# Infinity norm of rows: the last piece reduced alone, the other partial results joined beside it, and both stores issued by SyncE

## Chip, cores, metric

One core of one Trainium2 chip. The time is the device time in microseconds of one execution. Ratios are the mean time of one kernel's fast runs over the mean of the other's fast runs of the same rounds, so they are not quite the ratio of the medians quoted beside them.

The **tail**: the time from the landing of the last load (the last of the sixteen steps of its semaphore in the trace) to the end of the span. Its last part is the **closing block**: the event semaphores and drains that the engines run after the last store has landed.

## The reference

```python
x = np.random.randn(8192, 8192).astype(np.float32)
out = np.linalg.norm(x, ord=np.inf, axis=1)     # out[row] = max over 8192 columns of |x[row, col]|
```

## The kernel before

268 MB are loaded once, in tiles of 128 rows (or 256 rows as two per partition), and reduced along the row. VectorE takes the absolute maximum in one instruction. Near the end ScalarE and GpSimd help: ScalarE writes absolute values in place, GpSimd takes a maximum over them. The last tile is cut into six pieces of falling size, so that little work is left after the last load.

```python
    + [[(16384, (3712, 3680))], [(8192, (2016, 1984))]]
    + [[(3872, (1696,)), (1952, (832,)), (1024, (416,)), (544, (192,)), (384, ()), (416, ())]]
# (columns of a piece, (columns of it that ScalarE + GpSimd take)); the rest is VectorE's
WARM = {-2: (4, 4, 4), -1: (4,), 0: (4,), 1: (2,)}   # matmuls on zeros and ones after a piece
# ... cut ...
    last = single.tile([P, w_last + n_part_last], FP32)  # last piece AND 9 partial results, side by side
# ... cut: the loop over pieces ...
            if final:
                for r in range(2):
                    keep(nc.scalar.copy(sb_pairs[:, :, r], ps_pairs[r]))
                absmax(res[:, R - 1 :], last)             # 416 columns and 9 partials in one reduce
            elif u == len(TILES) - 1:
                # ... transposes of the finished rows, when h == 0 ...
                red = shared(last, w_last + n_part, buf, w, g)
                n_part += 1 + len(g)
                warm(red, WARM.get(h, ()))
# ... cut ...
    nc.tensor.transpose(ps_ones, res[:, X_ONE:], ident)   # [128, 4] -> [4, 128]
    keep(nc.scalar.copy(sb_ones, ps_ones))
    keep(nc.scalar.dma_start(out=out[X_ONE * P :].rearrange("(r p) -> r p", p=P), in_=sb_ones))
    nc.sync.dma_start(out=out[: X_ONE * P].rearrange("(g p r) -> g p r", p=P, r=2), in_=sb_pairs)
```

The results lie one per partition, 128 partitions wide; the transposes put them into rows, so that a store has few long runs. Pieces are counted from 0 below; piece 4 is the last but one, piece 5 the last.

## Time and profile before

| | before |
|---|---|
| time, median of 6 runs | 628.24 us (627.88 to 628.37) |
| profiled run, span | 628.42 us, 626.6 us |
| DMA | 268.47 MB, mean 428 GB/s over the span |
| last load lands | 623.11 us |
| tail | 3.50 us |

In the windows view, the columns are the stretch, its length, then the busy time (and instructions) of PE, PEld, DVE, ACT and POOL, then the granted clock, the DMA share and GB/s.

```profile
623.90:624.00 0.10, 0.07 (x1) 0.08 (x1) 0.00 (x0) 0.00 (x0) 0.00 (x0) 0.94 0.08 21
624.00:624.10 0.10, 0.10 (x1) 0.01 (x1) 0.00 (x0) 0.00 (x0) 0.00 (x0) 0.50 0.00 0
```

The clock falls to half at 623.99, while the last transpose (623.92 to 624.27) is running.

### The profile page before, as it was taken

Reading aid. Unit: us, or ns where it says so; the run is one execution under the profiler, and the core shown is the slowest. Engines: PE = TensorE matmul, PEld = TensorE weight load, DVE = VectorE, ACT = ScalarE, POOL = GpSimd, SP = SyncE. Lnnn points to the kernel's source line nnn. Section 1 sums busy time; section 2 is a strip of 40 time slices with the busy share of each in tenths; the row PEclk is TensorE's granted clock in tenths of the full one; section 3 lists DMA queues with packets and bytes.
Section 4 is the critical chain, followed back from the end, with each engine's and each line's share of the span. In section 5 each row is a group of like instructions: output and inputs, shape, how many; then the busy total and the mean of one; then the engine's idle time right before and its main releaser. Section 6 shows DMA issues by size and latency. Waiting matters only on the chain.

```text
span 626.6 us, 212 instructions
## 1 busy us (share of the span) xinstructions
PE 8.1 (1%) x15; PEld 3.0 (0%) x15; DVE 536.8 (86%) x40; ACT 15.6 (2%) x13; POOL 14.6 (2%) x16
## 2 busy tenths in 40 slices
PE   0000000000000000000000000000000000000005
PEld 0000000000000000000000000000000000000001
DVE  1938988889888899888898888988889888899888
ACT  0000000000000000000000000000000000000044
POOL 0000000000000000000000000000000000000026
PEclk9999999999999999999999999999999999999999
DMA  8999999999999999999999999999999999999997
GB/s 368 435 469 402 469 402 469 402 469 402 464 406 464 406 456 414 431 439 427 443 410 460 406 464 402 469 402 469 402 464 406 464 406 464 406 460 410 439 410 291
DMA packets 5669, 268.47 MB, mean 428 GB/s; under 512 B 643, under 2 KB 933, under 8 KB 1317
## 3 DMA queue, kind: packets, MB, share of 16 engines
q1 hardware_dynamic: 5661, 268.47, 99.2%
q10 hardware_dynamic: 8, 0.00, 0.0%
HBM read 268.44 MB, written 0.03 MB: 428 GB/s over the span
## 4 chain that ended last, share of the span: by engine, by line
DMA 71%; DVE 28%; SPq 0%; issue 0%; PE 0%; ACT 0%; DVEq 0%
DMA ring<-in_x_dram 71%; DVE res L75 28%; DVE last L75 1%; SPq L147 0%; PE ps_ones L189 0%; ACT sb_ones L190 0%; DVEq L75 0%
## 5 line engine op out<-in xcount | busy, mean ns | idle before, releaser
L75 DVE TENSOR_REDUCE res<-ring 128x2 f32<-128x16384 f32 (+1 forms) x32 | 525.4, 16420 | 86.8 <-DMA ring<-in_x_dram 86.8
L97 ACT ACTIVATE ring<-ring 128x3712 f32<-128x3712 f32 (+7 forms) x8 | 13.5, 1712 | 575.9 <-DMA ring<-in_x_dram 572.6
L82 POOL TENSOR_REDUCE part<-ring 128x1 int32<-128x3712 int32 (+3 forms) x4 | 10.1, 2563 | 586.0 <-ACT ring L97 586.0
L118 PE MATMUL ps_warm<-ident 128*128 128x512 f32 (+1 forms) x12 | 7.5, 764 | 614.5 <-DVE part L75 613.2
L118 PEld LDWEIGHTS ps_warm<-ident 128*128 128x128 f32 x12 | 2.7, 258 | 618.4 <-issue 615.3
L75 DVE TENSOR_REDUCE part<-ring 128x1 f32<-128x800 f32 (+1 forms) x2 | 5.5, 2748 | 0.1
L75 DVE TENSOR_REDUCE last<-ring 128x1 f32<-128x2176 f32 (+4 forms) x5 | 5.3, 1115 | 0.1
L82 POOL TENSOR_REDUCE last<-ring 128x1 int32<-128x1696 int32 (+3 forms) x4 | 3.3, 842 | 0.5 <-ACT ring L97 0.4
L110 ACT ACT_TABLE_LOAD x1 | 1.3, 1283 | 31.6 <-DVE res L75 31.6
L104 POOL MEMSET ident<- 128x128 f32 x1 | 0.2, 206 | 21.5 <-DVE res L75 21.5
L75 DVE TENSOR_REDUCE res<-last 128x1 f32<-128x425 f32 x1 | 0.6, 595 | 0.1
L161 ACT COPY sb_pairs<-ps_pairs 30x128 f32<-30x128 f32 x2 | 0.4, 252 | 0.0
L82 POOL TENSOR_REDUCE res<-part 128x1 int32<-128x3 int32 x2 | 0.4, 200 | 0.1
L167 PE MATMUL ps_pairs<-ident,res 128*30 128x128 f32 x2 | 0.4, 272 | 0.0
L189 PE MATMUL ps_ones<-ident,res 128*4 128x128 f32 x1 | 0.3, 348 | 1.7 <-DVE res L75 1.7
masks.py:199 POOL TENSOR_SCALAR_AFFINE_SELECT ident<-ident 128x128 f32<-128x128 f32 x1 | 0.3, 295 | 0.1
L190 ACT COPY sb_ones<-ps_ones 4x128 f32<-4x128 f32 x1 | 0.3, 255 | 1.5 <-PE ps_ones L189 1.5
L167 PEld LDWEIGHTS ps_pairs<-ident,res 128*30 128x30 f32 x2 | 0.2, 106 | 0.6 <-issue 0.6
L110 ACT ACTIVATE ident<-ident 128x1 f32<-128x1 f32 x1 | 0.2, 203 | 0.0
L211 POOL MEMSET const-float32-0.0<- 128x1 f32 x1 | 0.1, 99 | 0.2 <-issue 0.2
L211 POOL MEMSET const-bfloat16-1.0<- 128x1 bf16 x1 | 0.1, 102 | 0.0
L211 POOL MEMSET const-uint8-127<- 128x1 uint8 x1 | 0.1, 102 | 0.0
(2 smaller groups left out, 0.2 us busy)
## 6 DMA issues: line engine op xcount, KB each, us to landing
ring<-in_x_dram SPq DMA_DIRECT2D x3, 4096.0 KB, 21.6
ring<-in_x_dram SPq DMA_DIRECT2D x1, 1936.0 KB, 35.4
ring<-in_x_dram SPq DMA_DIRECT2D x1, 976.0 KB, 37.3
ring<-in_x_dram SPq DMA_DIRECT2D x1, 512.0 KB, 38.1
ring<-in_x_dram SPq DMA_DIRECT2D x30, 40.8
ring<-in_x_dram SPq DMA_DIRECT2D x1, 272.0 KB, 38.3
last<-in_x_dram SPq DMA_DIRECT2D x1, 208.0 KB, 38.3
ring<-in_x_dram SPq DMA_DIRECT2D x1, 192.0 KB, 38.3
```

Of the source, the lines that this page charges most:

```text
L75: return keep(nc.vector.tensor_reduce(out=dst, in_=src, axis=X, op=MAX, apply_absolute_value=True,))
L82: keep(pool.add_instruction(mybir.InstTensorReduce(name=nc.get_next_instruction_name(), ins=[pool.lower_ap(src.bitcast(INT32))], outs=[poo ...
L97: keep(nc.scalar.activation(buf[:, a : a + c], buf[:, a : a + c], ABS))
L104: not_before(nc.gpsimd.memset(ident, 0.0), after, "not before the first row is in")
L110: keep(nc.scalar.activation(ident[:, :1], ident[:, :1], ABS)),
L118: keep(nc.tensor.matmul(ps_warm[:, : w * P], lhsT=ident, rhs=ident.unsqueeze(1).to_broadcast([P, w, P]), start=True, stop=True,)),
L161: keep(nc.scalar.copy(sb_pairs[:, :, r], ps_pairs[r]))
L167: keep(nc.tensor.transpose(ps_pairs[r], both[:, :, r], ident))
L189: nc.tensor.transpose(ps_ones, res[:, X_ONE:], ident)
L190: keep(nc.scalar.copy(sb_ones, ps_ones))
L211: nc = _bacc.Bacc("TRN2", target_bir_lowering=False, num_devices=1)
```

## The change

Its intent: VectorE's last reduce should not wait for the nine partial results. It takes the last piece alone; GpSimd joins the nine meanwhile. The two columns are transposed one after the other, and VectorE takes the maximum of the two rows in one partition. The three finished single rows are transposed and copied earlier, so the last store is one row of 512 values; SyncE issues both stores. Some columns move between pieces, and two warm-ups are added.

```diff
-    + [[(16384, (3712, 3680))], [(8192, (2016, 1984))]]
-    + [[(3872, (1696,)), (1952, (832,)), (1024, (416,)), (544, (192,)), (384, ()), (416, ())]]
+    + [[(16384, (3712, 3680))], [(8192, (1952, 1920))]]
+    + [[(3872, (1728,)), (1952, (832,)), (1056, (448,)), (576, (224,)), (352, ()), (384, ())]]
-WARM = {-2: (4, 4, 4), -1: (4,), 0: (4,), 1: (2,)}
+WARM = {-2: (4, 4, 4), -1: (4,), 0: (4,), 1: (2,), 2: (2,), 4: (1,)}
 ... (tiles: parts apart from last; end[0..1], ps_end[0..1]; ps_ones and sb_ones in one partition)
             if final:
-                for r in range(2):
-                    keep(nc.scalar.copy(sb_pairs[:, :, r], ps_pairs[r]))
-                absmax(res[:, R - 1 :], last)
+                copied = keep(nc.scalar.copy(sb_ones[:, : (n_ones - 1) * P], ps_ones))
+                not_before(nc.sync.dma_start(out=..., in_=sb_pairs), copied, "out of the way of the loads")
+                absmax(end[0], last)
+                max_pool(end[1], parts)
 ... (piece 0: transposes of three single rows added; the pairs' copies moved here)
-    nc.tensor.transpose(ps_ones, res[:, X_ONE:], ident)
-    keep(nc.scalar.copy(sb_ones, ps_ones))
-    keep(nc.scalar.dma_start(out=..., in_=sb_ones))          # four rows of 128, ScalarE
-    nc.sync.dma_start(out=..., in_=sb_pairs)
+    keep(nc.tensor.transpose(ps_end[1], end[1], ident))
+    keep(nc.scalar.copy(sb_last, ps_end[1]))
+    keep(nc.tensor.transpose(ps_end[0], end[0], ident))
+    keep(nc.vector.tensor_tensor(out=sb_ones[:, (n_ones - 1) * P :], in0=ps_end[0], in1=sb_last, op=MAX))
+    nc.sync.dma_start(out=out[X_ONE * P :].rearrange("(o p) -> o p", o=1), in_=sb_ones)   # one row of 512
```

More of the change, by code (lines that the diff above doesn't have):

```diff
@@ L58 @@
     sb_pairs = single.tile([PAIRS, P, 2], FP32)
-    ps_ones = psum_pool.tile([n_ones, P], FP32)
-    sb_ones = single.tile([n_ones, P], FP32)
-    n_part_last = sum((w > sum(g)) + len(g) for w, g in TILES[-1][:-1])
-    w_last = TILES[-1][-1][0]
-    last = single.tile([P, w_last + n_part_last], FP32)
+    ps_ones = psum_pool.tile([1, (n_ones - 1) * P], FP32)
+    sb_ones = single.tile([1, n_ones * P], FP32)
+    sb_last = single.tile([1, P], FP32)
+    last = single.tile([P, TILES[-1][-1][0]], FP32)
+    parts = single.tile([P, sum(1 + len(g) for w, g in TILES[-1][:-1])], FP32)
+    end = [single.tile([P, 1], FP32, name=f"end{i}") for i in range(2)]
+    ps_end = [psum_pool.tile([1, P], FP32, name=f"ps_end{i}") for i in range(2)]
     def not_before(inst, other, why):
@@ L159 @@
             if final:
-                for r in range(2):
-                    keep(nc.scalar.copy(sb_pairs[:, :, r], ps_pairs[r]))
-                absmax(res[:, R - 1 :], last)
+                copied = keep(nc.scalar.copy(sb_ones[:, : (n_ones - 1) * P], ps_ones))
+                not_before(
+                    nc.sync.dma_start(
+                        out=out[: X_ONE * P].rearrange("(g p r) -> g p r", p=P, r=2),
+                        in_=sb_pairs,
+                    ),
+                    copied, "out of the way of the loads",
+                )
+                absmax(end[0], last)
+                max_pool(end[1], parts)
             elif u == len(TILES) - 1:
@@ L167 @@
                         keep(nc.tensor.transpose(ps_pairs[r], both[:, :, r], ident))
-                red = shared(last, w_last + n_part, buf, w, g)
+                    for i in range(n_ones - 1):
+                        one = res[:, X_ONE + i : X_ONE + i + 1]
+                        keep(nc.tensor.transpose(ps_ones[:, i * P : (i + 1) * P], one, ident))
+                red = shared(parts, n_part, buf, w, g)
+                if h == 0:
+                    for r in range(2):
+                        keep(nc.scalar.copy(sb_pairs[:, :, r], ps_pairs[r]))
                 n_part += 1 + len(g)
@@ L187 @@
                 warm(red, WARM.get(u - len(TILES) + 1, ()))
-    nc.tensor.transpose(ps_ones, res[:, X_ONE:], ident)
-    keep(nc.scalar.copy(sb_ones, ps_ones))
-    keep(nc.scalar.dma_start(
-        out=out[X_ONE * P :].rearrange("(r p) -> r p", p=P), in_=sb_ones
-    ))
-    nc.sync.dma_start(
-        out=out[: X_ONE * P].rearrange("(g p r) -> g p r", p=P, r=2), in_=sb_pairs
-    )
+    keep(nc.tensor.transpose(ps_end[1], end[1], ident))
+    keep(nc.scalar.copy(sb_last, ps_end[1]))
+    keep(nc.tensor.transpose(ps_end[0], end[0], ident))
+    keep(nc.vector.tensor_tensor(
+        out=sb_ones[:, (n_ones - 1) * P :], in0=ps_end[0], in1=sb_last, op=MAX
+    ))
+    nc.sync.dma_start(out=out[X_ONE * P :].rearrange("(o p) -> o p", o=1), in_=sb_ones)
 _INS = ['x']
```

## The prediction

> **What bounds the kernel now.** I read the page first (busy shares, DMA, chain), then the waits, then the last six microseconds of the timeline, and last the groups kept apart by shape.
>
> The page says that this is a load of 268 MB and little else:
>
> ```profile
> PE 8.1 (1%) x15; PEld 3.0 (0%) x15; DVE 536.8 (86%) x40; ACT 15.6 (2%) x13; POOL 14.6 (2%) x16
> DMA  8999999999999999999999999999999999999997
> DMA packets 5669, 268.47 MB, mean 428 GB/s; under 512 B 643, under 2 KB 933, under 8 KB 1317
> DMA 71%; DVE 28%; SPq 0%; issue 0%; PE 0%; ACT 0%; DVEq 0%
> ```
>
> The sixteen DMA engines are at nine tenths or more in every slice but the first and the last. VectorE (86% busy) waits for data between tiles; the 28% that the chain gives it are reduces that released a ring buffer while other loads kept the engines full. So some 622 us are the stream of loads, which the change doesn't touch: same bytes, same number of load instructions (39), the same two stores. Everything is decided after the last data. That end, in the timeline (start, duration, engine, line, tiles):
>
> ```profile
> 584.78 0.43 SPq L147 DMA_DIRECT2D last<-in_x_dram  x1
> ...
> 622.61 0.35 POOL L82 TENSOR_REDUCE last<-ring 128x1 int32<-128x192 int32 x1
> 622.64 0.54 DVE L75 TENSOR_REDUCE last<-ring 128x1 f32<-128x384 f32 x1
> 622.85 0.42 SPq L194 DMA_DIRECT2D out_dram<-sb_pairs  x1
> 623.27 0.59 DVE L75 TENSOR_REDUCE res<-last 128x1 f32<-128x425 f32 x1
> 623.92 0.08 PEld L189 LDWEIGHTS ps_ones<-ident,res 128*4 128x4 f32 x1 [2.05 <-DVE res L75]
> 623.92 0.35 PE L189 MATMUL ps_ones<-ident,res 128*4 128x128 f32 x1 [1.65 <-DVE res L75]
> 624.31 0.26 ACT L190 COPY sb_ones<-ps_ones 4x128 f32<-4x128 f32 x1 [1.48 <-PE ps_ones L189]
> 624.60 0.55 ACTq L191 DMA_DIRECT2D out_dram<-sb_ones  x1
> ```
>
> ```profile
> last<-in_x_dram SPq DMA_DIRECT2D x1, 208.0 KB, 38.3
> ...
> SPq L222 <- DMA out_dram<-sb_ones: 2.3, 1, 2.3
> ```
>
> The last piece is issued at 584.78 and takes 38.3 us, so it lands at 623.1 (623.11 in the trace's semaphore records). The last reduce could start there (elsewhere a released reduce starts 0.02 us after the landing: 623.13). It starts at 623.27, because it also reads the nine partial results, the last of them written by VectorE's own reduce that ended at 623.18. Then, in series: reduce 0.59, transpose, ScalarE's copy, ScalarE's store issue to 625.14, landing at 625.81 (0.67 after the issue; SyncE waits for it), and 0.8 us of closing barrier to 626.6. The path from last data to end is 3.5 us. Only this can move: **no outcome of 2% (12.6 us) is in reach.**
>
> **What the Trainium skill says.** "VectorE: DVE Perf Modes", section "The DRAIN you can't avoid", says that a same-engine read-after-write needs a semaphore, since the pipeline flush doesn't make it safe. The trace agrees and prices it: unrelated reduces overlap their predecessor by 0.08 us (622.719 to 622.636), the dependent one starts 0.09 us after it. "Perfetto Trace Analysis", section "Identifying Dependency Chains", says that a wait on several engines may get an extra event-semaphore instruction in front; one stands before this last reduce (623.14 to 623.22). "VectorE: DVE Perf Modes", section "The TRN2 errata", gives fp32 tensor_tensor as (N+151)/0.96 ns, which is 0.29 us for 128 elements: an estimate, as no trace of before has one. "DMA: Bandwidth & Descriptors", section "Issuing engines are not separate DMA queues", says that another issuer saves only sequencer time; here ScalarE's issue took 0.55 and SyncE's 0.42.
>
> **The change, part by part.** VectorE's reduces by shape:
>
> ```profile
> L75 DVE TENSOR_REDUCE part<-ring 128x1 f32<-128x4192 f32 x1 | 4.5, 4520 | 0.1
> L75 DVE TENSOR_REDUCE res<-last 128x1 f32<-128x425 f32 x1 | 0.6, 595 | 0.1
> L75 DVE TENSOR_REDUCE last<-ring 128x1 f32<-128x384 f32 x1 | 0.5, 543 | 0.0
> L75 DVE TENSOR_REDUCE last<-ring 128x1 f32<-128x352 f32 x1 | 0.5, 509 | 0.0
> L82 POOL TENSOR_REDUCE res<-part 128x1 int32<-128x3 int32 x2 | 0.4, 200 | 0.1
> L167 PE MATMUL ps_pairs<-ident,res 128*30 128x128 f32 x2 | 0.4, 272 | 0.0
> ```
>
> They fit 0.14 us plus 1.04 ns an element.
> (1) Split sizes. The tile before last gives VectorE 128 more elements (+0.13 us); it had ended at 617.74 with piece 0 landing at 617.82, so with the overlap of 0.08 piece 0 still starts on its landing, 617.84. Pieces 2, 3, 4 end 32, 64, 32 columns later in the row: at 16 KB for each 32 columns (x 4 B x 128 rows) and 428 GB/s they land 0.04, 0.08, 0.04 us later. Followed through: piece 1 620.20 to 621.52, piece 2 (608) 621.55 to 622.33, piece 3 (352) 622.25 to 622.76, piece 4 (352) 622.68 to 623.18. Nothing won or lost so far.
> (2) Last reduce. Its wait for the partials goes; it starts on the landing, 623.14 (0.14 earlier), and takes 0.54 for 384 elements instead of 0.59: it ends at 623.68, **0.19 earlier**.
> (3) Side branch. GpSimd's join of nine partials waits for piece 4's reduce (623.18) and its own part (about 623.08): start 623.26, 0.2 us as for three elements, to 623.46. Transpose about 623.52 to 623.82 (0.27 warm, as ps_pairs; up to 0.35, as ps_ones after its idle time). ScalarE copies it to one partition, 0.26 us, to about 624.12.
> (4) Main branch. Transpose of the last reduce from 623.73 to 624.01 or 624.08. So the joining tensor_tensor waits, by my sums, for ScalarE rather than for the transpose: start about 624.18, 0.29 us, to 624.47. The step before (transpose seen, copied) ended at 624.565: 0.1 us gained of the 0.19, as the side branch costs the rest.
> (5) Store on SyncE. Hop 0.03 (ScalarE to SyncE took that before the pairs' store), issue 0.42 to 624.92 against 625.14: **0.22 earlier** in sum. One row of 2 KB instead of four of 512 B; landing after the issue taken as the same 0.67: 625.59. The closing block follows unchanged.
> (6) Moved off the end: pairs' copies go behind piece 0's absolute values, where ScalarE idles 0.7 us (620.20 waits for its load); the copy of three finished rows (384 elements, about 0.46 us) ends near 623.0; the pairs' store is issued there, 0.15 later than now, and lands near 624.5, over a microsecond before the last one.
> Sum: 628.23 - 0.22 = **628.0 us**.
>
> **The rivals.**
> A: the side branch is the new bound and later than I think (GpSimd spans are rough; warm-up matmul, transpose, copy are in series). For: my sums give it 0.05 to 0.1 us over the main branch already. Against: GpSimd's 0.2 us for a tiny reduce came twice. With 0.2 us more, the gain is gone: 628.2.
> B: the chain is longer by a VectorE step with its event semaphore, and SyncE has two stores and the closing semaphore waits one after the other; before, it passed those waits while ScalarE issued. For: SyncE's closing waits cost some 0.25 us in all. Against: they fit into the 0.67 us of the store's landing. If not, 628.3.
> C: the join is hidden better than I think, and the single-row store is issued faster (SyncE issues took 0.33 to 0.43) or lands faster, being one piece instead of four. For: four rows arrived over 0.05 us. Then 0.3 to 0.45 us, 627.8 to 627.9.
> D: the new piece boundaries disturb the stream. Against: rows of 352 to 1056 elements are packets much like the 384 to 1024 now, and the queue is 38 us deep. Half a microsecond at most either way.
>
> **Range and chances.** 628.0 as the middle of A to C; the three times before lie within 0.15 us, and another load of the program may shift both kernels by a few tenths. Range 627.6 to 628.4. Even all rivals together are under 1 us of 628: 99% within 2%, half a per cent each side for a disturbed run.
>
> **What would show it.** The reduce of 384 should start within 0.03 us of its load's landing and end near 0.19 earlier, with no event semaphore on VectorE between it and the reduce before. The tensor_tensor's wait should be put down to ScalarE's copy (right) or to the second transpose (C). The chain's end should name SyncE's store, its issue near 0.42 us, with the landing 0.6 to 0.7 us after. Wrong would be: the span equal or longer with the last reduce earlier (A or B), a later landing of the last piece (D), or a pairs' store that lands last.

## The result, and the profile after

| | before | after |
|---|---|---|
| median of 6 runs | 628.24 us | 628.06 us (627.93 to 628.15) |
| ratio after / before | | 0.9998 (0.9985 to 1.0011): same |
| profiled run, span | 628.42 us, 626.6 us | 627.93 us, 626.1 us |
| last load lands | 623.11 us | 622.75 us |
| tail | 3.50 us | 3.38 us |

The page of the changed kernel, its DMA packets. The stream is what it was (before: 5669 packets, 268.47 MB, 428 GB/s):

```profile
DMA packets 5663, 268.47 MB, mean 429 GB/s; under 512 B 640, under 2 KB 926, under 8 KB 1311
```

The end in the timeline of the changed kernel (start, duration, engine, line, tiles, wait and what ended it):

```profile
622.31 0.52 DVE L78 TENSOR_REDUCE parts<-ring 128x1 f32<-128x352 f32 x1
622.61 0.42 SPq L165 DMA_DIRECT2D out_dram<-sb_pairs  x1
622.78 0.55 DVE L78 TENSOR_REDUCE end<-last 128x1 f32<-128x384 f32 x1
...
622.96 0.20 POOL L85 TENSOR_REDUCE end<-parts 128x1 int32<-128x9 int32 x1 [0.29 <-DVE parts L78]
...
623.22 0.27 PE L206 MATMUL ps_end<-ident,end 128*1 128x128 f32 x1
...
623.38 0.27 PE L208 MATMUL ps_end<-ident,end 128*1 128x128 f32 x1
623.53 0.26 ACT L207 COPY sb_last<-ps_end 1x128 f32<-1x128 f32 x1 [0.94 <-PE ps_end L206]
623.82 0.28 DVE L209 TENSOR_TENSOR sb_ones<-ps_end,sb_last 1x128 f32<-1x128 f32 x1 [0.48 <-ACT sb_last L207]
624.12 0.26 SPq L212 DMA_DIRECT2D out_dram<-sb_ones  x1
```

The waits of SyncE's queue in the changed kernel (waiter, what it waited for, us in total, times, longest):

```profile
SPq L212 <- DVE sb_ones L209: 1.0, 1, 1.0
SPq L238 <- DMA out_dram<-sb_ones: 0.7, 1, 0.7
```

The last reduce starts 0.02 us after its landing (622.754) and overlaps the end of the reduce before it, which ended at 622.83; that wait is gone, as intended, and no event semaphore stands before it on VectorE. GpSimd's join and the start of the first transpose now lie beside it, ScalarE's copy beside the second transpose. ScalarE's copy ends 0.03 us before the tensor_tensor starts. SyncE issues the last store and then waits for it.

Counted from the last landing, the first pair of profiles and the repeats (labels e10 and e1, told below) give this account in us:

| step | before | before again (e10) | after | after again (e1) |
|---|---|---|---|---|
| last reduce starts | 0.16 | 0.16 | 0.02 | 0.02 |
| last reduce ends | 0.76 | 0.76 | 0.58 | 0.58 |
| duration of a transpose | 0.35 | 0.27 | 0.27 | 0.27 |
| last store's issue starts | 1.48 | 1.41 | 1.37 | 1.36 |
| issue takes | 0.55 | 0.54 | 0.26 | 0.26 |
| last store lands | 2.69 | 2.60 | 2.51 | 2.50 |
| closing block, to the end | 0.81 | 0.81 | 0.86 | 0.86 |
| tail | 3.50 | 3.41 | 3.38 | 3.37 |

So two things in the first comparison are not yet explained: 0.36 us by which the last load landed earlier, and 0.12 us of tail where 0.22 was forecast. The experiments take these apart.

### The profile page after: what moved, and what is told of

Read it like the earlier page. It is cut to its first block, busy times and chain, and to the rows that moved or that the text cites. A ratio compares the mean times of both kernels' runs of the same rounds, so it can differ in the third digit from the quotient of the medians.

```text
span 626.1 us, 234 instructions
## 1 busy us (share of the span) xinstructions
PE 9.7 (2%) x23; PEld 4.0 (1%) x23; DVE 537.0 (86%) x41; ACT 15.9 (3%) x14; POOL 14.7 (2%) x17
## 2 busy tenths in 40 slices
DMA packets 5663, 268.47 MB, mean 429 GB/s; under 512 B 640, under 2 KB 926, under 8 KB 1311
## 3 DMA queue, kind: packets, MB, share of 16 engines
q1 hardware_dynamic: 5663, 268.47, 99.3%
## 4 chain that ended last, share of the span: by engine, by line
DMA 70%; DVE 29%; SPq 0%; issue 0%; PE 0%; ACT 0%
DMA ring<-in_x_dram 70%; DVE res L78 28%; DVE parts L78 1%; DVE part L78 1%; SPq L150 0%; PE ps_warm L121 0%; DVE sb_ones L209 0%; ACT sb_last L207 0%; PE ps_end L206 0%
## 5 line engine op out<-in xcount | busy, mean ns | idle before, releaser
L121 PE MATMUL ps_warm<-ident 128*128 128x512 f32 (+2 forms) x16 | 8.8, 675 | 614.0 <-DVE part L78 612.9
L78 DVE TENSOR_REDUCE parts<-ring 128x1 f32<-128x352 f32 (+3 forms) x5 | 5.3, 1106 | 0.0
L85 POOL TENSOR_REDUCE parts<-ring 128x1 int32<-128x1728 int32 (+3 forms) x4 | 3.4, 862 | 0.6 <-ACT ring L100 0.5
```

Of the source, the lines that this page charges most:

```text
L78: return keep(nc.vector.tensor_reduce(out=dst, in_=src, axis=X, op=MAX, apply_absolute_value=True,))
L85: keep(pool.add_instruction(mybir.InstTensorReduce(name=nc.get_next_instruction_name(), ins=[pool.lower_ap(src.bitcast(INT32))], outs=[poo ...
L121: keep(nc.tensor.matmul(ps_warm[:, : w * P], lhsT=ident, rhs=ident.unsqueeze(1).to_broadcast([P, w, P]), start=True, stop=True,)),
```

## The experiments

Each ran with five rounds against the kernel before on the same chip. There are twelve runs, all but e4 and e11 of versions meant to be correct; those two are wrong. No time ratio left the range 0.9997 to 1.0001, each with an interval of about 0.0013 either side, so the traces decide. In the tables, "issue" is the start of the last store's issue, "lands" is its landing, both from the last load's landing.

### e1: the changed kernel again; e10: the kernel before again

No edit.

> The changed kernel itself once more, unchanged, for a second profile. So far there is one profile of each kernel: from the last load's landing to the end of the span 3.50 us before and 3.38 after; but the last load also landed 0.36 us earlier after (622.75 against 623.11), and 0.17 of that is there at the very first load. Theory T (the change acts only after the last landing): the tail is again 3.38 within 0.03, while the landing of the last load may be anywhere from 622.7 to 623.2, as the stream is not the change's. Rival S (the changed program makes the stream itself faster): the last load lands at 622.75 within 0.05 again, and the sixteenth DMA engine trails the fifteenth by 0.05 us again (before: 0.16 at the first load, 0.31 at the last). Time: ratio to before 0.9995 to 1.0 either way.

> The kernel before, unchanged, for a second profile; its ratio to itself is the noise of the method. The first profile had a tail of 3.50 us with the one transpose at 0.348 us; the kernel before with only its last store on SyncE had 3.37 with that transpose at 0.272. Theory L (the TensorE clock at the very end is a matter of chance in this program: its mean clock was 0.998 in some of its runs and 1.0 in others): tail 3.42 to 3.44 with a transpose of 0.27, or 3.50 again with one of 0.35; nothing in between. Rival (the tail of before is 3.50 whatever the clock): 3.48 or more with a transpose of 0.27. The trailing sixteenth DMA engine: any amount from 0.05 to 0.4 us; time ratio 1.000 within 0.0003.

Measured: e1 628.07 us (before 628.11), ratio 0.9998 (0.9984 to 1.0011), tail 3.37. e10 628.06 us (the kernel before 628.10), ratio to itself 0.9999 (0.9987 to 1.0012), tail 3.41 with a transpose of 0.27: theory L, though 0.01 below its range.

**The clock.** The same end in the timeline of the kernel before, second profile, and its windows:

```profile
623.20 0.60 DVE L75 TENSOR_REDUCE res<-last 128x1 f32<-128x425 f32 x1
...
623.85 0.27 PE L189 MATMUL ps_ones<-ident,res 128*4 128x128 f32 x1 [1.65 <-DVE res L75]
624.16 0.26 ACT L190 COPY sb_ones<-ps_ones 4x128 f32<-4x128 f32 x1 [1.40 <-PE ps_ones L189]
624.45 0.54 ACTq L191 DMA_DIRECT2D out_dram<-sb_ones  x1
```

```profile
624.00:624.10 0.10, 0.10 (x1) 0.00 (x0) 0.00 (x0) 0.00 (x0) 0.00 (x0) 0.94 0.00 0
624.10:624.20 0.10, 0.03 (x1) 0.00 (x0) 0.00 (x0) 0.04 (x1) 0.00 (x0) 0.50 0.00 0
```

Here the clock falls at 624.09, 0.24 us after the transpose began, and the transpose has its 0.27. In the first profile it fell 0.06 us after the start, and the transpose took 0.35. The tail differs by 0.09, of which 0.08 is the transpose. So most of the 0.12 us between the first two profiles was the moment at which the clock fell. The Trainium skill ("TensorE: Matmul & The Clock Gate", Part 1) says that the window on which the gate decides runs freely and isn't tied to the kernel. The fourteen traces agree: in each, the clock is on record as full from another moment (616.05 to 619.20) and falls, once, 6.83 us (eight profiles) or 10.24 us (six) later, two or three times 3.41.

My expectation took a mean clock of 0.998 for cold; that failed: this run has 0.998 and a warm transpose. But the mean still sets a bound. If the clock falls once near the end, as in all the profiles, a run with 0.999 or more was, by an estimate from its span, at half clock for at most its last 1.9 us; the transpose ends 2.3 us before the end. Of the 32 runs of the kernel before with a clock in the experiments, 24 have 0.999 or more. So at most 8 can have met the slow transpose, and e10, one of the 8, did not: the 3.50 is the exception.

Against this warm profile the change is worth about 0.04 us of tail (3.41 to 3.37 and 3.38), not 0.12.

**The stream.** In e1 the last load landed at 623.02, not 622.75, so that profile's early landing is not fixed by the changed program, and rival S fails; the tail is theory T's. The first reduce, after the first load, started at 13.15 and 13.16 us in the two profiles of before, at 12.98 and 13.04 in those of after: part of the 0.36 us was there before anything that the change touches. It looks like scatter: e13 and e2, versions of before, have 12.84 and 13.31.

### e13: the kernel before with the added warm-ups

```diff
-WARM = {-2: (4, 4, 4), -1: (4,), 0: (4,), 1: (2,)}
+WARM = {-2: (4, 4, 4), -1: (4,), 0: (4,), 1: (2,), 2: (2,), 4: (1,)}
```

> The kernel before with the warm-up matmuls that the change adds after pieces 2 and 4, nothing else. Theory L: the transpose takes 0.27 us, so the tail is 3.42 to 3.44; the mean clock is 0.999 or 1.0 in every run, while the kernel before has 0.998 in some. Rival (the warm-up after piece 4 stands in front of the transpose): the transpose starts more than 0.06 us after the last reduce.

Measured: 628.11 us (before 628.10), ratio 1.0000 (0.9988 to 1.0013); transpose 0.27, starting 0.055 us after the last reduce; issue 1.41, lands 2.62, tail 3.43. As expected. It is a second value for before with a warm transpose: 3.41 to 3.43. Its mean clocks were 0.999 to 1.0.

### e5: the changed kernel without the added warm-ups

```diff
-WARM = {-2: (4, 4, 4), -1: (4,), 0: (4,), 1: (2,), 2: (2,), 4: (1,)}
+WARM = {-2: (4, 4, 4), -1: (4,), 0: (4,), 1: (2,)}
```

> The changed kernel without the added warm-up matmuls of pieces 2 and 4. Theory (they keep the TensorE clock up for the two transposes, 0.27 us each instead of the 0.35 of the kernel before): each transpose takes 0.35; as ScalarE's copy follows the first, the tensor_tensor starts about 0.08 us later after the last reduce (0.565 instead of 0.485), tail 3.46. Rival (the warm-up of piece 1 is enough, or the last warm-up is in the way of the first transpose): transposes 0.27 all the same, or the first one starts earlier after GpSimd's join than 0.05 us; tail 3.38 or less.

Measured: 628.05 us (before 628.07), ratio 1.0000 (0.9988 to 1.0012); both transposes 0.27; issue 1.37, lands 2.52, tail 3.39. The first theory fails: in this profile the clock stayed up without the added warm-ups. Whether they matter depends on where the stretches of 3.41 us lie. In the first pair of profiles they lie alike (full clock from 617.16 and 617.19). In before, TensorE was busy for 1.62 us of the stretch that ended at 623.99, and the clock fell; after the change, with the warm-ups and the added transposes, for 2.65 us of the one that ended at 624.01, and it stayed up. Over all profiles the busy share of that second stretch, by the trace's matmul records, was 0.28 to 0.57 where the clock then fell and 0.56 (this run) to 0.89 where it stayed. So the added work seems to hold the clock where a stretch ends at the wrong moment, and is not always needed; no run tests it at a fixed stretch.

### e2: the kernel before with only its last store on SyncE

```diff
-    keep(nc.scalar.dma_start(out=..., in_=sb_ones))
     nc.sync.dma_start(out=..., in_=sb_pairs)
+    keep(nc.sync.dma_start(out=..., in_=sb_ones))     # the same four rows of 512 B
```

> The kernel before with its last store (four rows of 512 B) issued by SyncE instead of ScalarE; nothing else. If the issuer alone sets the issue time, it takes 0.25 us as in the changed kernel (before 0.55), and the landing comes 1.15 us after its start (before 1.21). If the single row of 2 KB is what made the issue short, it takes 0.42 us as SyncE's other issues do. Tail: 3.50 plus the closing block's extra step of 0.06 if that comes from SyncE issuing the last store, less up to 0.06 of the earlier landing: 3.42 to 3.56. Rival S2 (a kernel without a DMA on ScalarE's queue has no trailing DMA engine): the sixteenth engine trails by 0.05 us, and the last load lands at 622.75. Against S2: it trails 0.15 or more at some loads, or by another amount.

Measured: 628.32 us (before 628.11), ratio 1.0001 (0.9988 to 1.0013). The end in its timeline:

```profile
624.25 0.25 ACT L190 COPY sb_ones<-ps_ones 4x128 f32<-4x128 f32 x1 [1.39 <-PE ps_ones L189]
624.53 0.28 SPq L194 DMA_DIRECT2D out_dram<-sb_ones  x1
```

Issue 1.39 and 0.28 long, lands 2.56, tail 3.37, with a warm transpose and no extra closing step. The tail is below the range I gave, which was built on the 3.50. One line of the change thus reaches the tail of the whole change, in one profile, and in part by chance. Of the 0.04 against e10, 0.02 came before the issue, where the edit changes nothing (the last reduce began at 0.15 instead of 0.16), and 0.02 between issue and landing. The issue is shorter by half because SyncE does it: 0.28 with four rows, 0.26 with one. The "trailing sixteenth DMA engine" of the expectations is the last of the sixteen steps of a load's semaphore. For the last load it came 0.40 us after the fifteenth, more than in any other profile, and in e3, which does use ScalarE's queue, 0.08: rival S2 fails.

### e3: the changed kernel with its last store on ScalarE

```diff
-    nc.sync.dma_start(out=out[X_ONE * P :].rearrange("(o p) -> o p", o=1), in_=sb_ones)
+    keep(nc.scalar.dma_start(out=out[X_ONE * P :].rearrange("(o p) -> o p", o=1), in_=sb_ones))
```

> The changed kernel with its last store (one row of 2 KB) issued by ScalarE; nothing else. If the issuer sets the issue time 0.55 us, if the single row does 0.25 to 0.3. Landing after issue start 1.21 as before or 1.15 as after. Tail 3.38 plus 0.05 to 0.1 less 0.06 if the closing block loses its extra step: 3.35 to 3.45. Rival S2 (ScalarE's queue brings a trailing engine): the sixteenth engine trails by 0.15 us and more, and the last load lands near 623.1.

Measured: 628.19 us (before 628.11), ratio 1.0000 (0.9987 to 1.0013); issue 1.38 and 0.49 long, lands 2.55, tail 3.41. With e2 this settles the store. The issue takes 0.49 to 0.55 on ScalarE and 0.25 to 0.28 on SyncE. But what counts is the time from the issue's start to the landing:

| | rows | issue | issue start to landing |
|---|---|---|---|
| before, e10, e13 (ScalarE) | 4 | 0.54 to 0.55 | 1.20 to 1.21 |
| e3 (ScalarE) | 1 | 0.49 | 1.17 |
| e2 (SyncE) | 4 | 0.28 | 1.17 |
| after, e1 (SyncE) | 1 | 0.26 | 1.15 |

The issue is 0.28 us shorter, the landing only 0.05 to 0.07 sooner, about half of it by the issuer (e2) and half by the single row (e3). The packets say why: the first one moves 0.80 us after the issue's start in before and 0.72 in after (0.74 in e3, 0.75 in e2); counted from the issue's end it is 0.25 and 0.47. The flight follows the start of the issue more nearly than its end, so adding a fixed flight to that end, as I did, is wrong. The extra closing step is in e3 too; it does not come from SyncE issuing.

### e4: GpSimd's join without piece 4's partial (wrong)

```diff
-                max_pool(end[1], parts)
+                max_pool(end[1], parts[:, :-1])
```

> The changed kernel, with GpSimd's join leaving out the partial result of piece 4 (wrong on purpose in those of the last 128 rows whose maximum lies in 352 of 8192 columns, about 4%), so that the side branch doesn't wait for piece 4's reduce. Theory (side branch ends last, by 0.12 us: the second transpose ended at 623.655, ScalarE's copy at 623.784): tensor_tensor starts 0.37 to 0.40 us after the end of the last reduce instead of 0.485, and the tail is 3.28 instead of 3.38. Rival (the transpose and event semaphores bind anyway): start stays at 0.46 or more and the tail at 3.36 or more.

Measured: 628.02 us (before 628.11), ratio 0.9997 (0.9985 to 1.0010); tensor_tensor at 1.05, tail 3.38. In its timeline:

```profile
622.85 0.20 POOL L85 TENSOR_REDUCE end<-parts 128x1 int32<-128x8 int32 x1
...
622.97 0.49 PE L121 MATMUL ps_warm<-ident 128*128 128x128 f32 x2 [0.18 <-DVE parts L78]
...
623.29 0.27 PE L206 MATMUL ps_end<-ident,end 128*1 128x128 f32 x1
```

The theory's numbers fail, but not for the rival's reason. The join now ends at 623.05, yet the transpose starts at 623.29, 0.46 us after the last landing, as in the changed kernel: the warm-up after piece 4, which stands ahead of it in TensorE's order, waits for piece 4's reduce in the same way.

### e11: the same, and without the warm-up after piece 4 (wrong)

```diff
-WARM = {... 1: (2,), 2: (2,), 4: (1,)}
+WARM = {... 1: (2,), 2: (2,)}
-                max_pool(end[1], parts)
+                max_pool(end[1], parts[:, :-1])
```

> The changed kernel with GpSimd's join leaving out piece 4's partial (wrong on purpose in about 4% of the last 128 rows) and without the warm-up matmul after piece 4. Leaving out the partial alone moved nothing (the first transpose then waited behind that warm-up), leaving out the warm-up alone neither (it then waited for GpSimd). Theory (either holds the side branch, and only both removed free it): first transpose starts near 0.27 us after the last landing instead of 0.46, its copy is done long before the second transpose, and the tensor_tensor starts at 0.95 to 0.99 instead of 1.06; tail 3.27 to 3.31. Rival (the main branch is as late anyway): tensor_tensor at 1.03 or more, tail 3.35 or more.

Measured: 627.95 us (before 628.10), ratio 0.9999 (0.9986 to 1.0011). In its timeline:

```profile
623.47 0.26 ACT L207 COPY sb_last<-ps_end 1x128 f32<-1x128 f32 x1 [0.72 <-PE ps_end L206]
...
623.52 0.27 PE L208 MATMUL ps_end<-ident,end 128*1 128x128 f32 x1
623.90 0.28 DVE L209 TENSOR_TENSOR sb_ones<-ps_end,sb_last 1x128 f32<-1x128 f32 x1 [0.44 <-PE ps_end L208]
```

Now the side branch is free: its first transpose starts at 0.28, and its copy is done at 0.84. Yet the tensor_tensor starts at 1.02, 0.11 us after the end given for the second transpose. The wait is now put down to that transpose. So the main branch alone needs 1.02 where the changed kernel has 1.06: the side branch costs it 0.05 us. Tail 3.34, a little above the range that I gave for the theory, below the rival's.

### e12: a correct version with an earlier side branch

```diff
-... (352, ()), (384, ())]]
+... (320, ()), (416, ())]]
-WARM = {... 1: (2,), 2: (2,), 4: (1,)}
+WARM = {... 1: (2,), 2: (2,)}
```

> A correct version meant to be better: the changed kernel with piece 4 of 320 and last piece of 416 columns instead of 352 and 384, and without the warm-up after piece 4. Piece 4 lands 0.04 us earlier and its reduce is 0.03 shorter, so the side branch comes 0.07 earlier; the main branch 0.03 later. Theory: copy of the side done at 0.96 after the last landing, second transpose done at 0.93; tensor_tensor starts at 0.99 to 1.03 instead of 1.06, tail 3.31 to 3.35. Rival (main branch needs its own 0.13 from transpose to tensor_tensor): start at 1.06, tail 3.38. Time ratio 0.9996 to 1.0.

Measured: 628.01 us (before 628.10), ratio 0.9997 (0.9984 to 1.0011); copy done at 0.99, second transpose at 0.93, tensor_tensor at 1.05, that is 0.11 after the transpose again; lands 2.50, tail 3.37. Both values lie between the theory's range and the rival's numbers. The profile puts the wait down to ScalarE's copy, the last of the two to end, but 0.06 us passed after it instead of the 0.03 of the other profiles: the copy comes early enough now and the main branch, 0.03 us later than with 384 columns, sets the start. The tail is that of e1, so these sizes win nothing more.

### e6: the changed kernel with the old piece sizes

```diff
-    + [[(16384, (3712, 3680))], [(8192, (1952, 1920))]]
-    + [[(3872, (1728,)), (1952, (832,)), (1056, (448,)), (576, (224,)), (352, ()), (384, ())]]
+    + [[(16384, (3712, 3680))], [(8192, (2016, 1984))]]
+    + [[(3872, (1696,)), (1952, (832,)), (1024, (416,)), (544, (192,)), (384, ()), (416, ())]]
```

> The changed kernel with the old split sizes (last piece 416, piece 4 384 columns). Theory: the last reduce still starts within 0.03 us of its landing, takes 0.03 longer (0.585 instead of 0.553); piece 4's reduce is 0.033 longer, but its load lands 0.04 us earlier, so the side branch is nearly the same against the last landing. Tail 3.37 to 3.42. Rival (the sizes are needed, VectorE would be late for the last landing): last reduce starts 0.05 us or more after the landing, tail 3.45 or more.

Measured: 628.11 us (before 628.07), ratio 1.0001 (0.9989 to 1.0014); last reduce starts at 0.02 and takes 0.585, tensor_tensor at 1.06, tail 3.38. As the theory said; the new sizes do nothing for the end.

### e7: the pairs' store not held back

```diff
-                not_before(nc.sync.dma_start(out=..., in_=sb_pairs), copied, "out of the way of the loads")
+                nc.sync.dma_start(out=..., in_=sb_pairs)
```

> The changed kernel without the order that holds the pairs' store back until the last rows' copy; it is issued as soon as the pairs are copied, about 619.5, beside the last loads. Theory (it is small, 30 KB in 430 GB/s, 0.07 us, but its packets stand in front of load packets): the last load lands up to 0.1 us later, the tail is unchanged at 3.38. Rival (two stores near each other on SyncE's queue cost the last one something): the last store's landing comes sooner after its issue than 1.15 us, tail 3.3 or less.

Measured: 627.97 us (before 628.07), ratio 1.0000 (0.9988 to 1.0013). The last load landed at 622.76, as early as in any profile; last store 1.15 from issue to landing; tail 3.40. Neither a delay of the loads nor a gain for the last store can be seen.

### e8: the join in 128 partitions

```diff
-    keep(nc.tensor.transpose(ps_end[1], end[1], ident))
-    keep(nc.scalar.copy(sb_last, ps_end[1]))
-    keep(nc.tensor.transpose(ps_end[0], end[0], ident))
-    keep(nc.vector.tensor_tensor(out=sb_ones[:, ...], in0=ps_end[0], in1=sb_last, op=MAX))
+    keep(nc.vector.tensor_tensor(out=res[:, R - 1 :], in0=end[0], in1=end[1], op=MAX))
+    keep(nc.tensor.transpose(ps_end[0], res[:, R - 1 :], ident))
+    keep(nc.scalar.copy(sb_ones[:, (n_ones - 1) * P :], ps_end[0]))
```

> The changed kernel with the join done in the 128 partitions by VectorE before a single transpose, instead of in one partition after two; the last reduce still takes its piece alone. Theory (a dependent step on VectorE costs a wait of 0.09 us and a fixed 0.16 to 0.2 us, so the early start is given back): last reduce starts within 0.03 us of its landing, tensor_tensor starts 0.1 after its end and takes 0.2, transpose 0.33 with its hop, copy 0.29 with its hop: store issued 0.9 to 0.95 us after the end of the last reduce instead of 0.79; tail 3.5 to 3.55, all of the gain gone. Rival (a small VectorE step costs under 0.1): store after 0.8, tail 3.4.

Measured: 628.08 us (before 628.07), ratio 1.0001 (0.9987 to 1.0014). In its timeline:

```profile
622.84 0.55 DVE L78 TENSOR_REDUCE end<-last 128x1 f32<-128x384 f32 x1
...
623.50 0.16 DVE L206 TENSOR_TENSOR res<-end,end 128x1 f32<-128x1 f32 x1
...
624.31 0.25 SPq L211 DMA_DIRECT2D out_dram<-sb_ones  x1
```

The early reduce wins 0.18 us (0.76 to 0.58), and the join gives it back: 0.11 of wait (623.39 to 623.50), the instruction's 0.16. The issue starts at 1.49, later than before (1.41). With the join in one partition the issue starts at 1.37: there VectorE's extra step takes ScalarE's place as the reader of PSUM. The tail, 3.43, is better than I expected by the closing block, which is back at 0.80.

That tells what the extra step goes with. SyncE's event semaphores in the closing block of the changed kernel, and of e8 (engine, line, count, shortest, median and longest ns, first and last start):

```profile
L238 SPq EVENT_SEMAPHORE  x7: 17/28/684, 624.4 to 626.1; - x7
```

```profile
L237 SPq EVENT_SEMAPHORE  x6: 17/28/672, 624.6 to 626.2; - x6
```

Five of the seven wait for the program's work, four of the six. The fourth waits for the last store; the fifth stands behind it, so it adds its 0.06 us. It is there in all nine profiles (after, e1, e3 to e7, e11, e12) in which a tensor_tensor in one partition comes last before the store, and in none of the five (before, e2, e8, e10, e13) in which ScalarE's copy does. The trace names the semaphores: in the nine SyncE closes on those of VectorE and GpSimd, in the five on ScalarE's alone, one fewer. Why the program is built so was not tested by itself.

## Why the prediction was right or wrong

**Right: the outcome and the bound.** 628.06 lies in 627.6 to 628.4, and the class is "same", as the change could move nothing but the 3.5 us after the last landing.

**Right: the wait removed, steps (1) and (2).** The last reduce starts at 0.02 instead of 0.16 and ends 0.18 us earlier (forecast 0.19). Piece sizes are neutral (e6). Step (6) holds as well: the pairs' store landed 1.2 us before the last one.

**Right in size: the side branch, steps (3) and (4).** The tensor_tensor was forecast 1.07 us after the last landing and came at 1.06; its wait is put down to ScalarE, as said. But the reason was too simple: I set the end of the copy (624.12) beside that of the second transpose (624.01 to 624.08) as if both had the same hop to VectorE. It is 0.03 from the copy and 0.11 from the transpose (e11, e12), so the side branch costs 0.05, not 0.1. GpSimd's join was later by 0.06 than I said, as its start after a VectorE reduce takes 0.14 (622.83 to 622.96), not 0.08. A transpose of 0.27 where I had allowed 0.30, and the hop of 0.03 where I had 0.06, made that up: to hit 1.06 this closely was luck. Rival A is thus refuted in its size.

**Wrong in size: the store, step (5).** I added 0.42 for the issue and a fixed 0.67 for the flight after it. The issue took 0.26 and the flight 0.89: from its start to landing 1.15 instead of 1.09. A shorter issue does not bring the landing forward by as much (e2, e3). Rival C's faster issue happened; its gain did not.

**Wrong: "the closing block follows unchanged".** It takes 0.86 instead of 0.81, for one more semaphore wait. Rival B named the place, but the cause is not that SyncE issues the last store (e2 has the short block, e3 the long one), nor are all waits exposed: three pass while the store is in flight, and the fourth is the wait for the store itself.

**Wrong, and not in any step: the starting point.** I took the tail of 3.50 as the kernel's own. 0.08 of it was a transpose that met the falling clock (e10, e13). The profile showed both 0.27 and 0.35, and I used them as a range for the new kernel, but not as a chance in the old one.

The sum in tail: forecast 3.28, measured 3.37 to 3.38; the difference is 0.06 in the store, 0.06 in the closing block, less 0.02 of an earlier issue. Against a warm before of 3.41, **the change is worth about 0.04 us** (0.03 to 0.06 between the two profiles of after and the two warm ones of before, e10 and e13): 0.18 from the reduce and 0.05 from the store, less 0.13 for the join (the time from the last reduce's end to the issue grew from 0.65 to 0.78) and 0.06 for the closing block.

The median fell by 0.18, close to the 0.22 that I forecast, but that agreement is chance. Over all rounds, 11 runs of the changed kernel average 628.07 and 38 of the kernel before 628.13, with standard deviations of 0.10 and 0.16, on several chips.

**Left open.** In the four profiles of before and its two near variants the last load landed at 623.04 to 623.14, in the ten of the changed form at 622.75 to 623.04. If the stream were really shorter by the difference of the means, 0.24, the times would show nearly 0.3 with the tail. Over all runs of both forms (51 and 48) the times differ by 0.07, with a standard error of 0.03. I have no step of the change that would reach the stream, and no run that shows one. Two things narrow it. At the fifteenth of the sixteen steps of the last load's semaphore the two groups overlap (622.74 to 623.12 and 622.68 to 622.96, means 0.09 apart); the rest is the last step, which trailed by 0.01 to 0.40 us in the four and 0.01 to 0.09 in the ten. And the four profiled executions were slow ones (628.25 to 628.42, where the 48 runs average 628.14). Why they fell so stays unexplained.

## What to carry to other kernels

When a kernel ends in a chain of small dependent steps, taking one wait away pays only what the replacement steps leave: write the chain down from the last landing to the end, old and new, with each handover (0.03 to 0.14 us here) as a term of its own, and the closing block too. Time a lone store from the start of its issue to its landing, not by the issue. And before explaining a tenth of a microsecond by a change, take the old kernel's profile twice.

## What the Trainium skill lacked or had wrong

- "DMA: Bandwidth & Descriptors", "Issuing engines are not separate DMA queues", says that another issuer saves the sequencer's issue time. For one small store at the end that time is not what is won: with the issuer alone changed (e2) the issue fell by 0.26 to 0.27 us, the time from its start to landing by 0.02 to 0.04. The page's fit of a fixed cost is for GpSimd's path; no page gives the time from issue to landing of a lone 2 KB store issued by SyncE or ScalarE: 1.15 to 1.21 us here.
- "TensorE: Matmul & The Clock Gate", Part 1, gives the cold state as coming after at least one idle window of about 3.4 us. The traces have that length, but the window need not be idle: in before TensorE was busy for 1.62 of the 3.41 us that ended with the fall, its last warm-up matmul only 1.7 us back (622.27 to 623.99). No page says how busy a window may be; here the shares before a fall reached 0.57.
- "VectorE: DVE Perf Modes", "The TRN2 errata": its tensor_tensor formula is stated as checked at 512 and 2048 elements alone. It comes within 5% at the sizes here: by estimate 0.29 and 0.16 us for 128 and 1 elements, measured 0.278 (one operand in PSUM) and 0.159.
- No page has the handover times: from the end given for a transpose 0.04 us to ScalarE, 0.11 to VectorE with two waits; from a VectorE reduce to GpSimd with two waits 0.14.
